# Three short gate/up pairs chained, and two more block products merged in the sixteen pairs after them

## The chip, the cores and the metric

The kernel runs on one core of a Trainium2 chip (trn2). The time is device microseconds from the start of an execution to its end. Engines are named as in the profile: PE (TensorE, matmul) with PEld (its weight loads), DVE (VectorE), ACT (ScalarE), POOL (GpSimd), SP (SyncE). PSUM is the accumulator memory that matmuls write; it has eight banks of 512 fp32 columns by 128 partitions, and the kernel allocates it in whole banks.

## The reference, cut to what matters

Two layers, each made of a first FFN, a token mix of three kinds of attention, and a second FFN, so four FFNs of one shape. All data are fp32.

```python
D_MODEL, SEQ, DEPTH, D_FF = 1024, 512, 2, 2816

def _swiglu(x, w1, w2):
    gt, up = jnp.split(x @ w1, 2, axis=-1)
    return (jax.nn.silu(gt) * up) @ w2

def reference(x, ...):
    for l in range(DEPTH):
        x = _layer_norm(DN_ALPHA * x + 0.5 * _swiglu(x, ffn1_w1[l], ffn1_w2[l]), ln1_g[l], ln1_b[l])
        mix = _token_mix(x, w_in[l], ...)
        x = _layer_norm(DN_ALPHA * x + mix, ln2_g[l], ln2_b[l])
        x = _layer_norm(DN_ALPHA * x + 0.5 * _swiglu(x, ffn2_w1[l], ffn2_w2[l]), ln3_g[l], ln3_b[l])
    return x
```

The change touches only `x @ w1` of `_swiglu`, followed by silu and the product.

## The kernel before, in words

**Precision.** An fp32 matmul is made of three in a rounded format (fp32r): every operand is split into a rounded part `hi` and a remainder `lo`, and hi·hi, hi·lo and lo·hi are added up in PSUM. ACT makes `hi` by a rounding copy (L160, L364, L369), DVE makes `lo` by a subtraction (L161, L365, L370). The activations `xx` (both parts, 512 tokens) stay in SBUF for a whole FFN; weights come by DMA as fp32 (`raw`) and are split as they come.

**One pair.** The first FFN product is computed in 22 pairs, f = 0 to 21: 128 gate columns and the 128 up columns that belong to them, for all 512 tokens. Pairs 0, 1 and 2 (`PLAIN`) are ordinary products (`proj`). From f = 3 on a pair is a 2x2 block product with seven block products in place of eight (Strassen's and Winograd's scheme): the tokens are cut into two halves of 256 (`H1`, `H2`), the 1024 inputs into two halves of four 128-row blocks. The left factors are sums and differences of weight blocks, made by DVE (`seven`, L348): g1 and g2 are the two halves of the gate weights, ua, ub, uc, ue and ud sums with the up weights. The right factors are blocks of the activations (p_, r_, s_) or of token sums (t1 to t4, tile `tz`). The products are named here by their left factors: P = g1·p_, then ua·t1, ub·t2, uc·t3, ud·t4, g2·r_ and ue·s_. The gate's first token half is P + g2·r_; the other three results share P and further sums.

**Two ways to run one block product.** `prod` (L402) issues twelve matmuls of 256 columns (four input blocks times hi·hi, hi·lo, lo·hi). `sided` (L410) lays the two parts of the right factor side by side: four matmuls of 512 columns give hi·hi in the first half of a bank and hi·lo in the second, then four of 256 columns add lo·hi to the first half. Its result lies in two halves that still have to be added (a "two-sided" sum); the diff calls this merged. Given two products, `sided` runs the 512s of the one, the 512s of the other, and then the 256s of both.

**Two ways to run a pair.** The short pairs f = 3, 4, 5 (below `HEAD` = 6, L341) go through `seven_products` (L419): three PSUM tiles, ga, pu and pv, each filled by two or one `prod`; sums are made by DVE (L432 to L439), partly from a copy `sn` that ACT makes (L428). No matmul there waits for a result of DVE or ACT of the same pair, except that g2 and ue at the end add to ga, which ACT copied long before. The sixteen pairs f = 6 to 21 go through `chained` (L442). There the running sum P + ub·t2 + ua·t1 + ue·s_ stays in one PSUM tile px, and its stages are copied out by ACT as they come: c1 after P (into half of the buffer t), cc after ub, the 512-wide cc after ua. uc and ud go to pw, g2 to py. ua, g2 and ue are merged, P, ub, uc and ud are not. ue and the evacuation of a pair are held back and run inside the next pair (`rest`, L482).

**Evacuation.** `evac` (L715) applies silu (ACT, L717) into one of two buffers t2[f % 2] and multiplies by the up half (DVE, L718). In `chained` the same buffer holds c1 until then.

**What sets the order.** PE's and POOL's instructions are issued in the order of the program text (`manual_schedule`, L89). DVE's and ACT's queues are ordered by a scheduler; copies and additions of `chained` have a raised priority there (L451, L455). An engine works through its queue in order, and waits between engines are derived from the tiles that the instructions read and write. PSUM tiles are taken in turn from a ring of eight banks (`ps`, L83): a tile gets the bank of the tile eight allocations earlier and waits until that has been read.

Of the kernel before, what the change touches and what calls it, by code (L numbers as in the profile page):

```python
# [10 lines left out]
F32 = mybir.dt.float32  # L11
F32R = mybir.dt.float32r
# [7 lines left out]
P = 128  # L20
S, D, F = 512, 1024, 2816
KD, KF, NB = D // P, F // P, S // P
# [44 lines left out]
def body(tc, a, out, depth=DEPTH):  # L67
# [13 lines left out]
    ring = [0]  # L81

    def ps(tag=None, name="ps", shape=(P, 512)):  # L83
        if tag is None:
            tag = PS_ALL[ring[0] % 8]
            ring[0] += 1
        return psp.tile(list(shape), F32, name=name, tag=tag, bufs=PS_TAGS[tag])
# [42 lines left out]
    nx = K()  # L130
# [210 lines left out]
    HEAD = 6  # L341
# [4 lines left out]
    H1, H2 = slice(0, 256), slice(256, 512)  # L346
# [55 lines left out]
    def prod(o, w, x, first=True):  # L402
        for k in range(4):
            hi, lo = w[0][:, k], w[1][:, k]
            vh, vl = x[0][:, k], x[1][:, k]
            for i, (wx, vx) in enumerate(((hi, vh), (hi, vl), (lo, vh))):
                nc.tensor.matmul(o, wx, vx, start=first and k == 0 and i == 0, stop=k == 3 and i == 2,  # L407
                                 skip_group_check=True)
# [30 lines left out]
        tt(ga[:, H2], ga[:, H2], v1, op=OP.add)  # L439
        return ga  # L440

    def chained(ws, tz, pl, u, held, end, t, evac):  # L442


        (g1, g2), (ua, ub, uc, ue), ud = ws
        (t1, t2, t3, t4) = [tz[:, i].rearrange("p k z s -> p z k s") for i in range(4)]
        two = lambda x: (x[:, 0], x[:, 1])
        p_, r_, s_ = [xx[:, :, k:k + 4, c] for k, c in ((0, H1), (4, H1), (4, H2))]

        def tt(*args):  # L450
            with tc.high_priority(100):  # L451
                nc.vector.tensor_tensor(*args, op=OP.add)

        def copy(o, x):
            with tc.high_priority(100):  # L455
                nc.scalar.activation(o, x, AF.Copy)  # L456

        px, pw, py = (ps(name=n) for n in ("px", "pw", "py"))
        cc = pl.tile([P, 768], F32, name="cc", tag="sn", bufs=1)
        prod(px[:, H1], g1, two(p_))  # L460
        c1 = t[:, H2]
        copy(c1, px[:, H1])
        prod(pw[:, H1], uc, two(t3))
        copy(pw[:, H2], pw[:, H1])
        if held:
            held.pop()()
        prod(px[:, H1], ub, two(t2), False)
        copy(cc[:, H1], px[:, H1])
        prod(pw[:, H1], ud, two(t4), False)
        y, x = (py, g2, r_, True), (px, ua, t1, False)  # L470
        if end:
            sided(x)
            sided(y)
        else:
            sided(y, x)
        copy(cc[:, 256:768], px)
        tt(c1, py[:, H2], c1)
        tt(py[:, H1], py[:, H1], c1)
        tt(u, pw, cc[:, 0:512])
        tt(u[:, H2], u[:, H2], cc[:, 512:768])  # L480

        def rest():  # L482
            sided((px, ue, s_, False))
            copy(t[:, H1], px[:, H2])
            tt(py[:, H2], px[:, H1], t[:, H1])
            evac(py)

        return rest

    def token_sums(k, tmp, th, tl):  # L490

# [213 lines left out]
    def ffn(l, w1, w2, which, xap, xa, wts, pend, done_prev, last, nxt, late=None):  # L705


        st = K()
        NA = KF - NTAIL
        plan = WIDE  # L710

        def hpart(f):
            return (st.ha, st.hb)[f >= NA][:, f - NA * (f >= NA)]

        def evac(f, pg, pu):  # L715
            t = st.t2[:, f % 2]
            g = nc.scalar.activation(t, pg, AF.Silu)  # L717
            st.last = g.ins, nc.vector.tensor_tensor(hpart(f), t, pu, op=OP.mult).ins  # L718

        hs, held = {}, []  # L720

        def h_parts(k, t):
            nc.scalar.activation(t[:, 0], hpart(k), AF.Copy)
            nc.vector.tensor_tensor(t[:, 1], hpart(k), t[:, 0].bitcast(F32), op=OP.subtract)
            hs[k] = t

        pts = staged(wts, pend)
        for tb in range(NB):
            nc.gpsimd.dma_start(x_sp[tb * P:(tb + 1) * P, :], xa[tb])
        done_prev()  # L730
        xap.release()
        st.w1p = nx.w1 = pool("w1p", side="right", reuse_waits="tile")
        more.n = 4
        with behind(lnq.sq):
            wp = [(wcols(w1, f * P), wcols(w1, F + f * P)) for f in PLAIN[2:]]

        for n, shape, dt, nb in (("hi", [P, KD, P], F32R, 2), ("lo", [P, KD, P], F32R, 2), ("ws", [P, KD, P], F32, 1),
                                 ("dh", [P, 4, P], F32R, 2), ("dl", [P, 4, P], F32R, 2), ("sn", [P, 768], F32, 1),
                                 ("v", [P, 256], F32, 1), ("raw", [P, KD, P], F32, 2)):
            st.w1p.tile(shape, dt, name=n, tag=n, bufs=nb)  # L740
        st.tz = st.w1p.tile([P, 4, 4, 2, 256], F32R, name="tz")
        th, tl = (st.tz[:, :, :, z] for z in range(2))
        tpl, nm, nb = (pre_t, "ws", 6) if late else (st.w1p, "raw", 2)
        lth = [token_sums(k, lambda: tpl.tile([P, KD, P], F32, name=nm, tag=nm, bufs=nb)
                          .rearrange("p a s -> p (a s)"), th, tl) for k in range(4)][-1]
        st.t = [(th[:, i], tl[:, i]) for i in range(4)]
        if late:
            late()
        fb = pool("fb", reuse_waits="tile")
        st.lnp = pool("lnp", reuse_waits="tile")  # L750
        st.t2 = st.lnp.tile([P, 2, S], F32, name="t2", tag="t2")
        fa = pool("fa", reuse_waits="tile")
        st.hb = fb.tile([P, NTAIL, S], F32, name="hb")
        st.ha = fa.tile([P, NA, S], F32, name="ha")

        ring[0] += 4
        for f in range(2, KF):
            if f not in PLAIN:
                ru = nx.w1.tile([P, KD, P], F32, name="raw", tag="raw", bufs=2) if f > 3 else None
                with behind(*(lth if f == PLAIN[-1] + 1 else lnq.parted if f < 6 else ())):  # L760
                    ws = seven(w1, f * P, F + f * P, nx.w1, ru, "half" if f < HEAD else "in place")
                with behind(*lnq.parted):
                    if f == PLAIN[-1] + 1:
                        evac(0, pts[0], pts[1])
                        evac(1, pts[2], pts[3])
                        for x in wp:
                            evac(*x)
                if f == KF - 1:
                    for k, n in zip(plan[1], ("hi", "lo")):
                        h_parts(k, wt.tile([P, KD, P], F32R, name=n, tag=n, bufs=3)  # L770
                                .rearrange("p (a b) c -> p a (b c)", a=2))
                if f < HEAD:
                    evac(f, seven_products(ws, st.t, nx.w1, hpart(f), 1), hpart(f))
                    continue
                held.append(chained(ws, st.tz, nx.w1, hpart(f), held, f == KF - 1, st.t2[:, f % 2], lambda p, f=f: evac(f, p, hpart(f))))
                if f == KF - 1:
                    held.pop()()
                continue
            wg, wu = wp.pop(0)
            pg, pu = ps(name="pg"), ps(name="pu")  # L780
            proj(pg, wg)
            proj(pu, wu)
            wp.append((f, pg, pu))
        nx.w1 = None
        st.w1p.tile([P, 88], F32, name="pad")
        st.w1p.release()
        accs = [[ps(name="acc") for _ in range(2)] for _ in range(NB)]
        short_rows(st, w2, accs, hs, h_parts, plan)
        xap, xa = alloc_xa(st.late if plan is WIDE else None)
        for tb in range(NB):  # L790
            nc.gpsimd.dma_start(xa[tb], x_sp[tb * P:(tb + 1) * P, :])
        hsp = pool("hsp", side="right", reuse_waits="tile")
        ln = LN(hsp, which, l, xa, 0.5, last)

        def wload(k):
            if k not in hs:
                h_parts(k, hsp.tile([P, 2, S], F32R, name="hs", tag="hs", bufs=5))
            return wrows(w2, k)

        wts, pend = rows_ln(KF, wload, lambda k: hs[k][:, 0], lambda k: hs[k][:, 1], ln, NA, fa.release, nxt,  # L800
                            plan[1][-1] + 1, accs)

        def done():
            nx_close()
            hsp.release()
            st.lnp.release()
            fb.release()

        return wts, pend, done, xap, xa
# [1145 lines left out]
    def late():  # L1955
        pre_t.release()
        tables(*tabs)
        init.release()
# [38 lines left out]
```

## Time and profile before

| | |
|---|---|
| runs | 2394.58, 2395.66, 2395.94 us; median 2395.66 |
| profiled execution | 2394.4 us; span of its instructions 2392.6 us |
| granted clock of TensorE | 0.999 of full speed |
| one FFN, three short pairs (899.9 to 930.1 us) | 30.2 us: PE 30.2 busy, DVE 26.3, ACT 14.6 |
| one FFN, sixteen pairs (930.1 to 1088.5 us) | 158.4 us: PE 158.4 busy, DVE 140.0, ACT 93.0 |

How to read it: times in the profile are us from the start of the span. A line such as `L407 PE MATMUL px<-xx,hi 128*128 128x256 f32 x12` is twelve matmuls of source line 407 that write tile px from xx and hi with 256 columns. What stands in brackets behind `<-` is the instruction that ended the idle time before. The chain that ended last is followed back from the last instruction; its pieces tell which engine sets the end at each moment. A matmul's length in the timeline (0.28 us for 256 columns) includes its way through the array; the distance from one start to the next is what it costs. The four FFNs begin their short pairs at about 49, 900, 1235 and 2087 us.

### The profile page before, as it was taken

What the parts mean: (1) busy time and instruction counts of PE and PEld (TensorE: products, weight loads), DVE (VectorE), ACT (ScalarE), POOL (GpSimd) and SP (SyncE); (2) the same over time, 40 slices, a digit from 0 to 9 for tenths busy, and PEclk for the clock granted to TensorE, in tenths of its full rate; (3) what the DMA queues carried; (4) which work ended last, traced back from release to release, by engine and by line L of the source; (5) the groups of instructions that cost most, each with busy time, mean ns of one, the idle gap of its engine ahead of it and who ended that gap; (6) DMA issues with size and microseconds to landing.
All of it is one profiled execution on the core that took longest, in us unless ns stands there. A gap on an engine that the chain in (4) does not pass through costs nothing.

```text
span 2392.6 us, 40932 instructions
## 1 busy us (share of the span) xinstructions
PE 2383.8 (100%) x15265; PEld 2113.8 (88%) x15265; DVE 1991.3 (83%) x3806; ACT 1326.6 (55%) x2537; POOL 344.6 (14%) x598
## 2 busy tenths in 40 slices
PE   9999999999999999999999999999999999999998
PEld 9999888888889989998899998878888898999987
DVE  7998975787688888998799989667777888999896
ACT  4565644577644545656445666445766445455563
POOL 2000312133321000001100002121333210000021
PEclk9999999999999999999999999999999999999999
DMA  6333975633165353437733349645322654433394
GB/s 205 109 111 103 243 203 160 177 95 87 45 160 140 115 161 110 116 103 207 203 116 111 110 140 207 197 131 153 99 78 60 158 135 149 125 106 110 102 237 142
DMA packets 407942, 330.23 MB, mean 138 GB/s; under 512 B 19208, under 2 KB 349336, under 8 KB 407744
## 3 DMA queue, kind: packets, MB, share of 16 engines
q1 hardware_dynamic: 380752, 261.83, 37.2%
q0 software_dynamic: 26992, 65.80, 11.9%
q8 instruction: 120, 1.97, 0.3%
q14 instruction: 78, 0.64, 0.1%
HBM read 300.26 MB, written 17.88 MB: 133 GB/s over the span
## 4 chain that ended last, share of the span: by engine, by line
PE 99%; DMA 0%; DVE 0%; POOL 0%; SPq 0%; issue 0%; POOLq 0%; ACT 0%; DVEq 0%
PE acc L574 13%; PE pw L407 8%; PE px L407 8%; PE acc L195 7%; PE pg L407 7%; PE pj L181 6%; PE pj L183 6%; PE pj L182 6%; PE px L414 5%; PE pu L407 3%; PE px L417 3%; PE py L414 2%; PE brp L182 2%; PE brp L181 2%; PE brp L183 2%; PE sN L1281 2%
## 5 line engine op out<-in xcount | busy, mean ns | idle before, releaser
L161 DVE TENSOR_TENSOR lo<-raw,hi 128x1024 fp32r<-128x1024 f32 x270 | 329.9, 1225 | 85.2 <-ACT hi L160 84.8
L160 ACT ACTIVATE hi<-raw 128x1024 fp32r<-128x1024 f32 x270 | 284.0, 1055 | 157.4 <-PE brp L182 36.3
L181 PE MATMUL pj<-xx,hi 128*128 128x512 f32 (+1 forms) x696 | 262.0, 376 | 0.2 <-ACT hi L1823 0.2
L183 PE MATMUL pj<-xx,lo 128*128 128x512 f32 (+1 forms) x696 | 250.5, 360 | 0.0
L182 PE MATMUL pj<-xx,hi 128*128 128x512 f32 (+1 forms) x696 | 250.5, 360 | 0.0
L574 PE MATMUL acc<-hi,xx 128*128 128x512 f32 x640 | 197.1, 389 | 0.0
L549 POOL DMA_DIRECT2D bt<-in_ffn_w_dram x32 | 40.4, 1273 | 935.6 <-DVE lo L161 935.3
L365 DVE TENSOR_TENSOR lo<-ws,hi 128x1024 fp32r<-128x1024 f32 x108 | 132.1, 1223 | 46.0 <-ACT hi L364 45.8
L183 PEld LDWEIGHTS pj<-xx,lo 128*128 128x128 f32 x696 | 131.5, 189 | 20.7 <-DVE lo L1824 0.2
L181 PEld LDWEIGHTS pj<-xx,hi 128*128 128x128 f32 x696 | 131.8, 189 | 16.2 <-issue 2.7
L182 PEld LDWEIGHTS pj<-xx,hi 128*128 128x128 f32 x696 | 132.2, 190 | 12.4 <-DVE xx L1909 0.2
L574 PEld LDWEIGHTS acc<-hi,xx 128*128 128x128 f32 x640 | 120.2, 188 | 24.9
L364 ACT ACTIVATE hi<-ws 128x1024 fp32r<-128x1024 f32 x108 | 114.1, 1056 | 49.3 <-DVE ws L387 15.8
L574 PE MATMUL acc<-lo,xx 128*128 128x512 f32 x320 | 124.6, 389 | 0.0
L407 PE MATMUL pg<-xx,hi 128*128 128x256 f32 x672 | 122.9, 283 | 0.0
L456 ACT ACTIVATE cc<-px 128x256 f32<-128x256 f32 (+1 forms) x128 | 62.5, 488 | 100.3 <-PE px L417 84.1
L407 PEld LDWEIGHTS pg<-xx,hi 128*128 128x128 f32 x672 | 106.2, 192 | 1.6
L456 ACT ACTIVATE t<-px 128x256 f32<-128x256 f32 x128 | 48.7, 380 | 84.4 <-PE px L407 47.0
L407 PE MATMUL pg<-xx,lo 128*128 128x256 f32 x336 | 95.2, 283 | 0.0
L407 PE MATMUL px<-xx,hi 128*128 128x256 f32 x512 | 94.9, 283 | 0.0
L407 PE MATMUL pw<-tz,hi 128*128 128x256 f32 x512 | 94.9, 283 | 0.0
L407 PE MATMUL pw<-tz,dh 128*128 128x256 f32 x512 | 94.9, 283 | 0.0
(482 smaller groups left out, 7184.1 us busy)
## 6 DMA issues: line engine op xcount, KB each, us to landing
raw<-in_ffn_w_dram SPq DMA_DIRECT2D x232, 512.0 KB, 3.9
raw<-in_w_in_dram SPq DMA_DIRECT2D x56, 512.0 KB, 4.0
raw<-in_w_gate_dram SPq DMA_DIRECT2D x48, 512.0 KB, 3.8
b<-in_ffn_w_dram SPq DMA_DIRECT2D x32, 512.0 KB, 7.4
bt<-in_ffn_w_dram POOLq DMA_DIRECT2D x32, 512.0 KB, 10.4
x_sp<-xa POOLq DMA_DIRECT2D x24, 512.0 KB, 6.5
xa<-x_sp POOLq DMA_DIRECT2D x24, 512.0 KB, 4.6
ks<-hl SPq DMA_DIRECT2D x96, 128.0 KB, 2.4
```

The source lines that it names most:

```text
L160: lnq.hi = nc.scalar.activation(hi[:, c], raw[:, c], AF.Copy).ins
L161: lnq.lo = nc.vector.tensor_tensor(lo[:, c], raw[:, c], hi[:, c].bitcast(F32), op=OP.subtract).ins
L181: nc.tensor.matmul(o, hi[:, k], vh, start=first, stop=False)
L182: nc.tensor.matmul(o, hi[:, k], vl, start=False, stop=False)
L183: nc.tensor.matmul(o, lo[:, k], vh, start=False, stop=last)
L195: nc.tensor.matmul(o, x(k)[:, t], y[:, c], start=first and i == 0, stop=last and i == 2, skip_group_check=True)
L364: pa = nc.scalar.activation(hi, x, AF.Copy)
L365: pv = tt(lo, x, hi.bitcast(F32), op=OP.subtract)
L407: nc.tensor.matmul(o, wx, vx, start=first and k == 0 and i == 0, stop=k == 3 and i == 2, skip_group_check=True)
L414: nc.tensor.matmul(o, w[0][:, k], x[:, :, k], start=first and k == 0, stop=False, skip_group_check=True)
L456: nc.scalar.activation(o, x, AF.Copy)
L574: nc.tensor.matmul(o[t], u[:, k, s], v[:, c], start=first and j == 0 and i == 0, stop=False, skip_group_check=True)
```

## The change

`seven_products` is no longer used by the FFN: f = 3, 4 and 5 go through `chained` too, with `merged=""`, so that all seven products are `prod`. There P and the running sum use the second half of the bank whose first half takes g2 (`x = px[:, H2]` with `px = py`), and one ring position is skipped. ACT copies c1 after P, cc after ub and after ua; ue then adds straight onto the second half, so that the held-back part has no copy and no addition. The order is P, g2, (ue and evacuation of the pair before), ub, uc, ua, ud.

For f = 6 to 21 `merged` is "AEGBP". P is merged (its copy c1 becomes 512 wide and fills t), and B (ub) is merged and issued in one `sided` call with ue of the pair before. Both copies of the running sum, after ub and after ua, are 512 wide and go to a 1024-wide cc. The gate's first half is folded from two-sided sums by `tt(c1, py, c1)` and `tt(py[:, H1], c1[:, H1], c1[:, H2])`; u gets two 512-wide additions. The tiles are taken in the order py, pw, px where it was px, pw, py. The order is P, uc, (ue of the pair before with B, its evacuation), ud, g2 with ua. The tiles `sn` (768) and `v` (256) give way to `cc` (1024).

```diff
-    def chained(ws, tz, pl, u, held, end, t, evac):
+    def chained(ws, tz, pl, u, held, t, evac, merged, end):
...
-        px, pw, py = (ps(name=n) for n in ("px", "pw", "py"))
-        cc = pl.tile([P, 768], F32, name="cc", tag="sn", bufs=1)
-        prod(px[:, H1], g1, two(p_))
-        c1 = t[:, H2]
-        copy(c1, px[:, H1])
-        prod(pw[:, H1], uc, two(t3))
+        def product(o, w, x, first=False):
+            prod(o, w, (x[:, 0], x[:, 1]), first)
+
+        py, pw = ps(name="py"), ps(name="pw")
+        if merged:
+            px = ps(name="px")
+        else:
+            px = py
+            ring[0] += 1
+        xc = H1 if merged else H2
+        x = px[:, xc]
+        cc = pl.tile([P, 1024], F32, name="cc", tag="cc", bufs=1)
+        sides = cc.rearrange("p (z i s) -> p z i s", z=2, i=2)
+        two = lambda y: y.rearrange("p (z s) -> p z s", z=2)
+        c1 = t if "P" in merged else t[:, H2]
+
+        def first():
+            if "P" in merged:
+                sided((px, g1, p_, True))
+                copy(c1, px)
+            else:
+                product(x, g1, p_, True)
+                copy(c1, x)
+
+        def last():
+            if not merged:
+                tt(py[:, H1], py[:, H1], c1)
+            elif "P" in merged:
+                tt(c1, py, c1)
+                tt(py[:, H1], c1[:, H1], c1[:, H2])
...
+            tt(u, pw, cc[:, 0:512])
+            if merged:
+                tt(u, u, cc[:, 512:1024])
+
+        if merged:
+            first()
+            product(pw[:, H1], uc, t3, True)
+            copy(pw[:, H2], pw[:, H1])
+            e = held.pop() if held else None
+            b = (px, ub, t2, False)
+            if e and e[0]:
+                sided(e[0], b)
+                e[1]()
+            else:
+                if e:
+                    e[1]()
+                sided(b)
+            copy(sides[:, :, 0], two(px))
+            product(pw[:, H1], ud, t4)
+            y, a_ = (py, g2, r_, True), (px, ua, t1, False)
+            if end:
+                sided(a_)
+                sided(y)
+            else:
+                sided(y, a_)
+            copy(sides[:, :, 1], two(px))
+            last()
+
+            def rest():
+                copy(t[:, H1], px[:, H2])
+                tt(py[:, H2], px[:, H1], t[:, H1])
+                evac(py)
+
+            held.append(((px, ue, s_, False), rest))
...
+            return
+        first()
+        product(py[:, H1], g2, r_)
+        if held:
+            held.pop()[1]()
+        product(x, ub, t2)
+        copy(cc[:, H1], x)
+        product(pw[:, H1], uc, t3, True)
         copy(pw[:, H2], pw[:, H1])
...
+        product(x, ua, t1)
+        copy(cc[:, H2], x)
+        product(pw[:, H1], ud, t4)
+        last()
 
         def rest():
-            sided((px, ue, s_, False))
-            copy(t[:, H1], px[:, H2])
-            tt(py[:, H2], px[:, H1], t[:, H1])
+            product(x, ue, s_)
             evac(py)
 
-        return rest
+        held.append((None, rest))
...
-                if f < HEAD:
-                    evac(f, seven_products(ws, st.t, nx.w1, hpart(f), 1), hpart(f))
-                    continue
...
+                chained(ws, st.tz, nx.w1, hpart(f), held, st.t2[:, f % 2], lambda p, f=f: evac(f, p, hpart(f)),
+                        "" if f < HEAD else "AEGBP", f == KF - 1)
```

More of the change, by code (lines that the diff above doesn't have):

```diff
@@ L440, in seven_products @@
         return ga
-    def chained(ws, tz, pl, u, held, end, t, evac):
+    def chained(ws, tz, pl, u, held, t, evac, merged, end):
         (g1, g2), (ua, ub, uc, ue), ud = ws
         (t1, t2, t3, t4) = [tz[:, i].rearrange("p k z s -> p z k s") for i in range(4)]
-        two = lambda x: (x[:, 0], x[:, 1])
         p_, r_, s_ = [xx[:, :, k:k + 4, c] for k, c in ((0, H1), (4, H1), (4, H2))]
@@ L456, in copy @@
                 nc.scalar.activation(o, x, AF.Copy)
-        px, pw, py = (ps(name=n) for n in ("px", "pw", "py"))
-        cc = pl.tile([P, 768], F32, name="cc", tag="sn", bufs=1)
-        prod(px[:, H1], g1, two(p_))
-        c1 = t[:, H2]
-        copy(c1, px[:, H1])
-        prod(pw[:, H1], uc, two(t3))
-        copy(pw[:, H2], pw[:, H1])
[L465 to L480, printed above, removed]
+        def product(o, w, x, first=False):
[6 more added lines that the diff above has]
+            ring[0] += 1
@@ new lines, in last @@
+        def last():
[5 more added lines that the diff above has]
+            else:
+                tt(c1, py[:, H2], c1)
+                tt(py[:, H1], py[:, H1], c1)
+            tt(u, pw, cc[:, 0:512])
[20 more added lines that the diff above has]
+                sided(y)
+            else:
+                sided(y, a_)
[6 more added lines that the diff above has]
+            held.append(((px, ue, s_, False), rest))
+            if end:
+                e = held.pop()
+                sided(e[0])
+                e[1]()
+            return
@@ L737, in ffn @@
         for n, shape, dt, nb in (("hi", [P, KD, P], F32R, 2), ("lo", [P, KD, P], F32R, 2), ("ws", [P, KD, P], F32, 1),
-                                 ("dh", [P, 4, P], F32R, 2), ("dl", [P, 4, P], F32R, 2), ("sn", [P, 768], F32, 1),
-                                 ("v", [P, 256], F32, 1), ("raw", [P, KD, P], F32, 2)):
+                                 ("dh", [P, 4, P], F32R, 2), ("dl", [P, 4, P], F32R, 2), ("cc", [P, 1024], F32, 1), ("raw", [P, KD, P], F32, 2)):
             st.w1p.tile(shape, dt, name=n, tag=n, bufs=nb)
@@ L771, in ffn @@
                                 .rearrange("p (a b) c -> p a (b c)", a=2))
-                if f < HEAD:
-                    evac(f, seven_products(ws, st.t, nx.w1, hpart(f), 1), hpart(f))
-                    continue
-                held.append(chained(ws, st.tz, nx.w1, hpart(f), held, f == KF - 1, st.t2[:, f % 2], lambda p, f=f: evac(f, p, hpart(f))))
-                if f == KF - 1:
-                    held.pop()()
+                chained(ws, st.tz, nx.w1, hpart(f), held, st.t2[:, f % 2], lambda p, f=f: evac(f, p, hpart(f)),
+                        "" if f < HEAD else "AEGBP", f == KF - 1)
                 continue
```

## The prediction

> **What bounds the kernel now.** The page first: span, busy line, chain of waits.
>
> ```profile
> span 2392.6 us, 40932 instructions
> PE 2383.8 (100%) x15265; PEld 2113.8 (88%) x15265; DVE 1991.3 (83%) x3806; ACT 1326.6 (55%) x2537; POOL 344.6 (14%) x598
> ...
> PE 99%; DMA 0%; DVE 0%; POOL 0%; SPq 0%; issue 0%; POOLq 0%; ACT 0%; DVEq 0%
> ```
>
> The matrix engine is busy without a break and is 99% of the chain that ended last. So the change can gain only by making the matmul stream itself shorter, and any wait that it puts into that stream is paid in full. The second view is therefore the chain in order of time, over one of the 64 pairs (16 in each of four FFNs) that the change merges further. Columns: start, length, line, count of matmuls.
>
> ```profile
> 958.74 1.44 PE px L407 x12
> 960.18 1.44 PE pw L407 x12
> 961.62 0.93 PE px L414 x4
> 962.55 0.47 PE px L417 x4
> 963.02 1.44 PE px L407 x12
> 964.45 1.44 PE pw L407 x12
> 965.89 0.93 PE py L414 x4
> 966.82 0.91 PE px L414 x4
> 967.73 0.47 PE py L417 x4
> 968.21 0.48 PE px L417 x4
> 968.69 1.44 PE px L407 x12
> ```
>
> In order: P (g1), uc, the last product ue of the pair before, B (ub), ud, then g2 and ua merged, and the next P. One pair takes 968.69 - 958.74 = 9.95 us. A plain product is twelve 256-column matmuls, 1.44 us, 0.12 each. A merged one is four 512-column and four 256-column matmuls: 0.93 + 0.47 = 1.40 us on the activations (xx), 0.91 + 0.48 = 1.39 on the token sums (tz). The third view is the same chain in the three short pairs ahead.
>
> ```profile
> 900.06 2.87 PE pg L407 x24
> 902.93 2.88 PE pu L407 x24
> 905.81 1.44 PE pv L407 x12
> 907.25 5.76 PE pg L407 x48
> 913.01 2.88 PE pu L407 x24
> ```
>
> Seven plain products back to back, 2.87 + 2.88 + 1.44 + half of 5.76 = 10.07 us; the matmul engine waits nowhere.
>
> **The merge in the 16 pairs.** P goes from 1.44 to 1.40 and B from about 1.435 (963.02 to 964.45 is 1.43) to 1.39; uc, ue, ud, g2 and ua keep their matmuls. The new pair is 1.40 + 1.44 + 1.40 + 1.39 + 1.44 + 2.79 = 9.86, so 0.09 less, and 64 x 0.09 = 5.8 us. That is the whole possible gain, 0.24%. The bounds are the rounding of these rows: 0.08 to 0.10, 5.1 to 6.4 us.
>
> The price of a matmul is what this hangs on. Four 256s of P (0.48) become two 512s' worth of time (0.93 / 2 = 0.465), so only what each matmul costs beyond its columns is saved. The Trainium skill, "TensorE: Matmul & The Clock Gate", section "Wait — 56ns, not 53.3ns?", says that a warm matmul costs its columns at 2.4 GHz and about 2.5 ns more. By that, merging away four matmuls saves an estimated 10 ns a product and 1.3 us over 128 products. It returns below beside a rival.
>
> What the merge adds beside the stream: the copy of P into t and the copy of B become 512 wide, and so do two additions. Groups by line, with the mean in ns:
>
> ```profile
> L364 ACT ACTIVATE hi<-ws 128x1024 fp32r<-128x1024 f32 x14 | 14.8, 1054 | 1.2 <-DVE ws L380 1.0
> ...
> L456 ACT ACTIVATE cc<-px 128x512 f32<-128x512 f32 x16 | 9.6, 598 | 25.9 <-PE px L417 25.9
> ...
> L456 ACT ACTIVATE cc<-px 128x256 f32<-128x256 f32 x15 | 5.7, 377 | 2.2 <-PE px L407 1.6 <-ACT t L456 0.7
> ```
>
> ```profile
> L452 DVE TENSOR_TENSOR ha<-pw,cc 128x512 f32<-128x512 f32 x12 | 8.2, 683 | 0.1
> L452 DVE TENSOR_TENSOR t<-py,t 128x256 f32<-128x256 f32 x16 | 6.7, 420 | 3.5 <-PE py L417 3.4
> ...
> L452 DVE TENSOR_TENSOR ha<-ha,cc 128x256 f32<-128x256 f32 x12 | 5.0, 416 | 0.0
> ```
>
> ScalarE gets 2 x (0.598 - 0.377) = 0.44 us a pair, VectorE 2 x 0.265 = 0.53. How much room they have is one row of the windows over 14 pairs:
>
> ```profile
> core 0: us, PE busy (x) PEld busy (x) DVE busy (x) ACT busy (x) POOL busy (x), PEclk, DMA share, GB/s
> ...
> 938.68:1078.11 139.43, 139.43 (x1010) 132.00 (x1009) 127.58 (x183) 82.81 (x139) 0.00 (x0) 1.00 0.37 110
> ```
>
> VectorE is busy 127.58 / 14 = 9.11 us a pair and would be busy 9.64 of 9.86; ScalarE goes from 5.9 to 6.4. No DMA is added or moved, and cc takes the memory of sn and v. ScalarE's addition is hidden by its own idle time. VectorE's is hidden only while 0.2 us a pair are left; that is the second rival.
>
> Some waits exist already. Where the copy of B was late, the matmul engine waited for it (start, length, engine, line):
>
> ```profile
> 978.52 0.40 PE L407 MATMUL px<-xx,hi 128*128 128x256 f32 x2
> ...
> 985.56 0.78 PEld L414 LDWEIGHTS py<-xx,hi 128*128 128x128 f32 x4
> 985.68 1.09 PE L414 MATMUL py<-xx,hi 128*128 128x512 f32 x4
> ...
> 986.17 0.37 ACT L456 ACTIVATE cc<-px 128x256 f32<-128x256 f32 x1
> ...
> 986.60 0.77 PEld L414 LDWEIGHTS px<-tz,hi 128*128 128x128 f32 x4 [0.26 <-ACT cc L456]
> ...
> 986.96 0.59 ACT L717 ACTIVATE t<-py 128x512 f32<-128x512 f32 x1
> ```
>
> and in the chain
>
> ```profile
> 986.77 1.03 PE px L414 x4
> ```
>
> The copy ended at 986.54, the next weight load began at 986.60, and the group took 1.03 instead of 0.91: 0.12 us lost. With a copy longer by 0.22 the same lateness loses about 0.34. A second one is new: the tiles are now taken in the order py, pw, px from eight banks, so a pair's px gets the bank of py two pairs back, which is free only after that pair's silu. Here the silu starts 986.96 - 978.52 = 8.4 us after P's first matmul. It follows ue, whose end the merge moves back by the 0.91 of B's 512s, so it would end at 8.4 + 0.9 + 0.6 = 9.9, against a pair of 9.86. A few pairs would lose some 0.2 us. I take 0.8 us in all for both, with 0 and 3 as ends, since most copies come in time. The merge alone is then -5.8 + 0.8 = -5.0 us.
>
> **The three short pairs.** They keep 84 matmuls of 0.12 us, so nothing is gained on the path. VectorE loses five additions and gets two, which is worth nothing while it is not waited for. What is new is the order: P into the second half of py, copy c1 out of it by ScalarE, then g2 into the first half of the same tile. In the code nothing of g2 depends on c1. But whether the halves count as separate, a row shows:
>
> ```profile
> 914.05 0.69 DVE L390 TENSOR_TENSOR raw<-raw,ws 128x512 f32<-128x512 f32 x1
> 916.00 0.42 DVE L432 TENSOR_TENSOR v<-pu,sn 128x256 f32<-128x256 f32 x1 [1.26 <-PE pu L407]
> ```
>
> v reads only the first half of pu. That half was complete 12 matmuls after 913.01, at about 914.5, and VectorE stood idle from 914.74, yet v began at 916.00, just after the second half (915.89). A reader thus waits for a write to the other half of its tile. I take it that a writer waits for a reader likewise; no row shows that direction. The Trainium skill, "PSUM — Partial Sum Buffer", section "PSUM bank collisions raise a hardware error", speaks against this change here: it counts a read by ScalarE and a write by TensorE in one bank as a collision whichever columns they touch, and tells authors to guard by bank.
>
> The price of one such wait, from f = 6, whose P and c1 are plain now too:
>
> ```profile
> 931.57 0.40 PE L407 MATMUL pw<-tz,hi 128*128 128x256 f32 x2
> ...
> 931.83 0.38 ACT L456 ACTIVATE t<-px 128x256 f32<-128x256 f32 x1 [0.51 <-PE px L407]
> ```
>
> The next product begins at 931.57, the copy of P at 931.83 and ends at 932.21: 0.64 after. From a copy's end to the weight load it is 0.06 (986.54 to 986.60), from there to the matmul 0.12 (985.56 to 985.68). So 0.64 + 0.06 + 0.12 = 0.82 us, in three pairs of four FFNs: 12 x 0.82 = 9.8 us. The low end is a copy that starts at once, 0.56 each, 6.7 us; the high end, half of the copies behind a weight split that has just begun on ScalarE (1.05), 9.8 + 6 x 1.05 = 16 us. I take 0.82, since in the row ScalarE stood waiting for the copy. Behind the waiting g2 stands the whole matmul queue.
>
> One of the 12 costs more. c1 goes to half of the buffer t, which an earlier pair's silu and product use:
>
> ```profile
> 48.78 0.40 PE L407 MATMUL pg<-xx,hi 128*128 128x256 f32 x2
> ...
> 50.20 1.28 DVE L718 TENSOR_TENSOR ha<-t,pj 128x512 f32<-128x512 f32 x2
> ```
>
> In the first FFN, P of the first short pair ends at 48.78 + 1.44 = 50.22, but the product that reads t ends at 51.48. The copy then ends at about 51.9, and the wait is 1.9 instead of 0.82: 1.1 us more. The other copies of the short pairs have a product of 1.44 us ahead of the matmul that needs them, more than 0.82, and cost nothing.
>
> **Sum.** -5.8 + 0.8 + 9.8 + 1.1 = +5.9 us. The profiled execution is 2394.4 us (span 2392.6, 1.8 around it), so 2400.3; it lies 1.3 below the median of 2395.66, and against that median the sum gives 2401.6 us, 0.25% slower. What this measurement can tell from no change is about 0.2%, 4.8 us: below 2390.9 is faster, above 2400.5 slower. With the ends named, this case runs from 2397 (0.56 a wait, nothing else late) to 2409.
>
> **The rivals.**
> *Halves are separate for a writer* (not slower). If g2 does not wait for c1, the 9.8 and the 1.1 go: c1 then has g2, 1.44 us, as cover. The result is 2395.7 - 5.0 = 2390.7, on the edge of faster. For it: no row shows a writer waiting. Against it: the row of v. It decides as soon as the matmul after the short P starts 0.12 after the last one. 22%.
> *VectorE becomes the bound.* At 9.64 of 9.86 us it has almost no slack, and it takes its work in order. If half of its present idle time of (139.43 - 127.58) / 14 = 0.85 us stays as waiting in order, a pair lasts 9.64 + 0.42 = 10.06, 0.2 more than its matmuls, in 14 x 4 pairs 11 us; with the short pairs' part even 2412. It decides once splits of the next pair are late at its P. Against it: an engine that is behind arrives later and waits less, and the short pairs give VectorE some time back. 15%.
> *Merging saves hardly anything.* If P and B as 512s cost as much as their 256s, because the stream has to step between two stretches of xx or because weight loads set the pace, the 5.8 us go and the time is 2407.4. It decides when four 512s reach 0.96. The rows of 0.93 and 0.91, of products merged the same way already, speak against it: 5%. By the estimate from the Trainium skill's page "TensorE: Matmul & The Clock Gate" above it would be 2401.6 + 5.8 - 1.3 = 2406; the trace disagrees with that page, with 0.04 to 0.05 us a product where it gives 0.01.
>
> **How the numbers follow.** The likeliest case has 58% and gives 2401.6; of it 36 points lie above 2400.5 and 22 within 0.2%. Separate halves: 22%, 12 faster and 10 the same. VectorE 15% and the dear merge 5%, slower. Faster 0.12, same 0.32, slower 0.56. The likeliest case's own range is 2397 to 2409; to hold 8 in 10 it must reach down to the separate halves, 2390, and up to 2410, which leaves out most of the VectorE case and the lowest of the separate halves.
>
> **What would show it.** Right: in the short pairs an idle time of 0.7 to 0.9 us ahead of g2, 12 times, released by ScalarE's copy into t, and one near 1.9 in the first FFN; in the 16 pairs 9.86 from P to P. Wrong: g2 following P without a gap (first rival); pairs of 10 us and more with waits on splits or additions (second); pairs still at 9.95 without waits (third); silu ahead of P's waits in many pairs, which I priced at nearly nothing.

## The result

The changed kernel takes 2409.82 us (median of 6 runs, 2408.73 to 2410.37) and the kernel before 2394.48 (6 runs beside them, 2393.81 to 2395.94): ratio 1.0063, 95% interval 1.005 to 1.0076. That is 15.3 us slower. The profiled executions differ by the same: span 2408.1 against 2392.6.

The page of the profile after, its first lines and the line of the chain by engine:

```profile
span 2408.1 us, 39973 instructions
...
PE 2383.7 (99%) x14753; PEld 2085.1 (87%) x14753; DVE 2018.3 (84%) x3770; ACT 1365.4 (57%) x2573; POOL 345.4 (14%) x598
...
PE 11%; DVE 2%; ACT 1%; issue 0%; POOL 0%; POOLq 0%; DVEq 0%; ACTq 0%
```

There are 512 matmuls fewer, 4 in each of 128 products. The busy time of PE hardly fell, because part of each wait counts as busy: a matmul's recorded length (0.28 us) reaches beyond the 0.12 after which the next can start, so that a wait of 0.63 shows as 0.47 idle in the timeline below. The chain could be followed back over 11% of the span only, so it is no use here. What PE waited for is the better view (what waited, for what: us in total, times, longest). After:

```profile
PE py L407 <- ACT t L455: 9.3, 12, 2.5
PE px L414 <- ACT cc L455: 3.0, 8, 0.5
PE py L407 <- ACT cc L455: 1.6, 1, 1.6
PE pj L181 <- ACT hi L1876: 1.2, 1, 1.2
...
PE pw L407 <- ACT pw L455: 0.3, 2, 0.2
```

and before, where beside one wait at the kernel's very start this is all:

```profile
PE pj L181 <- ACT hi L1823: 0.2, 1, 0.2
```

The 12 waits of py for t are the ones that were forecast, g2 behind the copy c1 out of its own bank: one in each short pair of each feed-forward network (FFN). Three other kinds of wait for a ScalarE copy are there too.

By stage, from the first matmul of the short pairs to the first after the sixteenth merged pair, as the matmuls' starts give it:

| us | FFN 0 | FFN 1 | FFN 2 | FFN 3 | sum |
|---|---|---|---|---|---|
| before | 189.56 | 189.57 | 189.57 | 189.57 | 758.27 |
| after | 194.75 | 192.63 | 192.25 | 193.78 | 773.41 |

These stages hold 15.1 of the 15.5 us between the spans. Another 0.3 is at the start of the kernel (pj behind hi), ahead of the first short pair; elsewhere the two traces run alike. Within the stages the matmul gaps of the short pairs add up to 15.0 us, and the sixteen merged pairs come out even.

One nominal wait, timeline of after (start, length, engine, line, operation, and in brackets the idle time and what ended it):

```profile
927.69 0.28 PE L407 MATMUL py<-xx,lo 128*128 128x256 f32 x1
928.44 0.50 PE L407 MATMUL py<-xx,hi 128*128 128x256 f32 x2 [0.47 <-ACT t L455]
...
928.00 0.38 ACT L455 ACTIVATE t<-py 128x256 f32<-128x256 f32 x1 [0.92 <-PE py L407]
```

g2 should have started 0.12 after 927.69. It starts 0.06 after the copy's end (928.38), 0.63 late, and its first two matmuls take 0.50 together where 0.40 is usual: 0.73 in all.

A merged pair that nothing disturbs, same view:

```profile
967.54 1.09 PE L414 MATMUL px<-xx,hi 128*128 128x512 f32 x4
968.47 0.63 PE L417 MATMUL px<-xx,lo 128*128 128x256 f32 x4
968.94 0.40 PE L407 MATMUL pw<-tz,hi 128*128 128x256 f32 x2
...
977.40 0.86 PE L414 MATMUL px<-xx,hi 128*128 128x512 f32 x3
```

From P to P it is 977.40 - 967.54 = 9.86 us, and P's parts are 0.93 (to 968.47) and 0.47. But three pairs of every FFN are longer: 10.61, 10.40 and 10.14 to 10.17. The longest, with ScalarE's queue behind it:

```profile
961.80 1.06 ACT L160 ACTIVATE hi<-raw 128x1024 fp32r<-128x1024 f32 x1
962.77 0.36 ACT L455 ACTIVATE t<-px 128x256 f32<-128x256 f32 x1
963.03 1.05 ACT L364 ACTIVATE hi<-raw 128x1024 fp32r<-128x1024 f32 x1
963.98 1.05 ACT L160 ACTIVATE hi<-raw 128x1024 fp32r<-128x1024 f32 x1
964.93 0.59 ACT L455 ACTIVATE cc<-px 128x512 f32<-128x512 f32 x1
...
964.00 1.09 PE L414 MATMUL py<-xx,hi 128*128 128x512 f32 x4
965.57 1.19 PE L414 MATMUL px<-tz,hi 128*128 128x512 f32 x4 [0.48 <-ACT cc L455]
```

Two splits of L160 stand in ScalarE's queue here, and the clean pair after it has none. Four pairs of each FFN carry two such splits, and the three late ones are among them; the pairs with one or none are not late. The copy of B comes last behind them, and ua, due 0.93 after 964.00, starts 0.64 late and loses 0.10 more at its start.

### The profile page after: what moved, and what is told of

Read it like the earlier page. It is cut to its first block, busy times and chain, and to the rows that moved or that the text cites. A ratio compares the mean times of both kernels' runs of the same rounds, so it can differ in the third digit from the quotient of the medians.

```text
span 2408.1 us, 39973 instructions
## 1 busy us (share of the span) xinstructions
PE 2383.7 (99%) x14753; PEld 2085.1 (87%) x14753; DVE 2018.3 (84%) x3770; ACT 1365.4 (57%) x2573; POOL 345.4 (14%) x598
## 5 line engine op out<-in xcount | busy, mean ns | idle before, releaser
L161 DVE TENSOR_TENSOR lo<-raw,hi 128x1024 fp32r<-128x1024 f32 x270 | 330.5, 1227 | 89.8 <-ACT hi L160 89.4
L160 ACT ACTIVATE hi<-raw 128x1024 fp32r<-128x1024 f32 x270 | 283.5, 1054 | 156.2 <-PE brp L182 36.3
L364 ACT ACTIVATE hi<-ws 128x1024 fp32r<-128x1024 f32 x108 | 114.4, 1059 | 48.8 <-DVE ws L387 15.4
L414 PE MATMUL px<-tz,hi 128*128 128x512 f32 x512 | 139.0, 393 | 3.0 <-ACT cc L455 3.0
L414 PE MATMUL px<-xx,hi 128*128 128x512 f32 x512 | 139.8, 394 | 0.0
L455 ACT ACTIVATE cc<-px 128x512 f32<-128x512 f32 x128 | 76.1, 595 | 95.3 <-PE px L417 94.3
L414 PEld LDWEIGHTS px<-tz,hi 128*128 128x128 f32 x512 | 94.7, 188 | 28.1 <-ACT cc L455 8.2
L407 PE MATMUL pw<-tz,dh 128*128 128x256 f32 x608 | 112.9, 283 | 0.3 <-ACT pw L455 0.3
L407 PE MATMUL pw<-tz,hi 128*128 128x256 f32 x608 | 112.2, 282 | 0.0
L365 DVE TENSOR_TENSOR lo<-raw,hi 128x1024 fp32r<-128x1024 f32 x76 | 92.8, 1221 | 18.9 <-ACT hi L364 18.9
L455 ACT ACTIVATE t<-px 128x512 f32<-128x512 f32 (+1 forms) x128 | 62.3, 486 | 68.7 <-PE px L417 48.2
```

The costliest lines, as they stand in the source:

```text
L160: lnq.hi = nc.scalar.activation(hi[:, c], raw[:, c], AF.Copy).ins
L161: lnq.lo = nc.vector.tensor_tensor(lo[:, c], raw[:, c], hi[:, c].bitcast(F32), op=OP.subtract).ins
L364: pa = nc.scalar.activation(hi, x, AF.Copy)
L365: pv = tt(lo, x, hi.bitcast(F32), op=OP.subtract)
L414: nc.tensor.matmul(o, w[0][:, k], x[:, :, k], start=first and k == 0, stop=False, skip_group_check=True)
```

## The experiments

The kernel before was run beside each; its medians lie between 2394.28 and 2394.68. The two theories at the start: the loss is g2 waiting for the copy in its own bank (the forecast); or the sixteen pairs lose as well, to VectorE or to the merge itself.

**The short pairs back to before, the merged sixteen kept.**

```diff
+                if f < HEAD:
+                    evac(f, seven_products(ws, st.t, nx.w1, hpart(f), 0), hpart(f))
+                    continue
```

> Short pairs f = 3 to 5 back to the seven separate products, the sixteen pairs merged as in the change. Theory (the short pairs carry the whole loss, 15.0 us of the 15.5 us between the two spans, because g2 waits for the copy out of its own bank, and the sixteen pairs come out even): 2394 to 2396 us; if the three late copies of an FFN come from a backlog that the short pairs leave, they go as well and it is 2388 to 2390. Rival (the loss comes from the sixteen pairs, VectorE or their copies): still above 2404.

Here `seven_products` keeps its copy and the sum v in the tile cc instead of the tiles sn and v; its short pairs take 30.2 us an FFN as before.

2399.43 us, ratio 1.002 (1.001 to 1.0029): between the two. So most of the loss is the short pairs' own, but the merge alone, which I had put at 5 us of gain, costs 4.9. What PE waits for:

```profile
PE pw L407 <- DVE lo L365: 3.9, 3, 1.3
PE px L414 <- ACT t L459: 1.7, 2, 0.8
...
PE px L414 <- ACT cc L459: 0.7, 2, 0.5
```

The products wait for VectorE's half of a weight split (lo) and for late copies out of px.

**The short pairs as changed, the sixteen as before.**

```diff
+                if f < HEAD:
+                    chained(ws, st.tz, ..., "", False)
+                else:
+                    chained_old(ws, st.tz, ...)
```

> Short pairs as in the change, the sixteen pairs as before (P and B plain). Theory: the short pairs alone cost 15 us, 2409 to 2411 us. Rival (the merge in the sixteen pairs is to blame): 2394 to 2398.

2410.90 us, ratio 1.007 (1.0055 to 1.0085): the short pairs alone carry 16.4 us, in the profiled execution 1.2 of it through a slower clock behind the longest wait (the last section shows it). PE's waits are those of the changed kernel without the late copies out of px:

```profile
PE py L407 <- ACT t L455: 8.8, 12, 2.5
PE py L407 <- ACT cc L455: 2.3, 2, 1.3
```

The two halves of the change cost 4.9 and 16.4 by themselves and 15.3 together. They don't add up, since each moves the order of VectorE's and ScalarE's work, and so which copy is late.

**The running sum of the short pairs in a bank of its own, same order.**

```diff
-            px = py
-            ring[0] += 1
+            px = ps(name="px")
...
-        product(py[:, H1], g2, r_)
+        product(py[:, H1], g2, r_, True)
...
+            copy(py[:, H2], x)
```

> As the change, but in the short pairs the running sum lies in a third bank and not in the bank of g2; same order of the products, and one 256-wide copy more at the evacuation, off the path. Theory (bank): the twelve waits ahead of g2 (11.2 us in the trace) go, apart from about 1.4 us in the first FFN where the copy comes later than g2 can cover; the waits for a late copy ahead of ua and ud (about 2.5 us) stay: 2399 to 2401 us. Rival (the copy is late for its data, the bank does not matter): the waits move to ub, and it stays at 2406 to 2410.

2396.18 us, ratio 1.0009 (1.0 to 1.0018): 13.6 us come back, more than I expected. All 12 waits ahead of g2 are gone; what is left are late copies:

```profile
PE px L414 <- ACT cc L455: 2.9, 8, 0.5
...
PE px L407 <- ACT t L455: 1.1, 1, 1.1
```

The last is in the first FFN, where ub and not g2 is now the next product that needs the copy; it shows that c1 comes late there whatever stands behind it.

**The same bank, with uc between the copy and g2.**

```diff
         first()
+        product(pw[:, H1], uc, t3, True)
+        copy(pw[:, H2], pw[:, H1])
         product(py[:, H1], g2, r_)
...
-        product(pw[:, H1], uc, t3, True)
-        copy(pw[:, H2], pw[:, H1])
+        product(pw[:, H1], ud, t4)
```

> As the change, but the order in the short pairs is P, uc, g2, (ue before), ub, ud, ua: the bank of P and g2 is shared as in the change, and uc, 1.44 us into another bank, stands between. Theory (bank, and only the neighbourhood of P and g2): the waits of 0.63 to 1.1 us are covered, the first FFN keeps about 1.3 us: 2398 to 2401 us. Rival (copy late for its data): 2406 to 2410.

2394.17 us, ratio 0.9998 (0.9989 to 1.0008): even with the kernel before, 15.7 us under the change. PE's waits for copies:

```profile
PE py L407 <- ACT t L455: 1.4, 1, 1.4
...
PE py L407 <- ACT cc L455: 0.8, 1, 0.8
```

Eleven of the twelve waits are gone without another bank. A product of 1.44 us into another bank is cover enough; so the price was not the copy, but that g2 stood directly behind it. Not all of the 15.7 us is this, however: by the matmuls' starts the short pairs give back 11.4, and 3.6 come from the sixteen merged pairs, which were not edited. Their late copies cost about 0.3 twice in each FFN, and 0.15 a third time in three of the four, where in the change they cost 0.74, 0.53 and 0.28.

**The copy c1 issued twice.**

```diff
                 copy(c1, x)
+                copy(c1, x)
```

> The changed kernel with the first block product's copy of the short pairs issued twice (12 more copies of 256 columns, 0.28 to 0.38 us each on ScalarE, out of the bank that g2 writes). Bank theory: g2 waits for the second copy too, each of the 12 waits grows by 0.3 to 0.4 us, and the time goes from 2409.8 to 2413 to 2415. Rival (the wait ends with something other than the copy): 2409 to 2411.

2415.43 us, ratio 1.0089 (1.0075 to 1.0102): 5.6 more than the change. The nominal waits grew from 0.63 to 1.05, and the long one of the first FFN from 2.70 to 3.12; the middle ones, 1.10 before, have no split ahead of their two copies now and take 1.05. One such wait:

```profile
930.82 0.80 ACT L455 ACTIVATE t<-py 128x256 f32<-128x256 f32 x2 [0.92 <-PE py L407]
...
930.50 0.28 PE L407 MATMUL py<-xx,lo 128*128 128x256 f32 x1
931.67 0.50 PE L407 MATMUL py<-xx,hi 128*128 128x256 f32 x2 [0.89 <-ACT t L455]
```

The copies end at 931.62 and g2 starts 0.05 later, though its own half of the tile was never copied. With the two runs before, this shows that g2 waits for every copy out of the other half. Whether the bank makes it wait, or the way in which this program derives its waits from tiles, no run tells apart, since a PSUM tile is a whole bank in all of them. The sum of all waits rose by 3.6 us only, since the middle ones did not grow; 1.5 more are a stretch at a slower clock in the first FFN.

**Less work on VectorE, in the merged sixteen alone and in the whole change.** Both leave out the second addition of the up sum.

```diff
-            if merged:
-                tt(u, u, cc[:, 512:1024])
```

First with the short pairs of before:

> The kernel with short pairs as before and the merged sixteen, with the second addition of the up sum left out in the sixteen pairs (64 additions of 512 columns; this part of the sum is missing from the output). Theory that VectorE's load makes the merge come out even: without 64 x 0.66 us on VectorE the weight splits come earlier, the waits of ua and uc for VectorE's lo and for late copies shrink, and the time falls from 2399.4 to 2389 to 2393. Rival theory (the loss is the two-sided products' own, on TensorE, or ScalarE's queue alone): 2398 to 2400.

2392.5 us, ratio 0.9992 (0.9983 to 1.0001): 6.9 us less than with the addition. The waits for lo are gone. The addition was also a reader of cc, but in neither trace does a copy into cc wait for VectorE, so the effect is put down to the load. Then in the changed kernel:

> The changed kernel with the second addition of the up sum left out in the sixteen pairs (64 additions of 512 columns on VectorE; that part of the sum is missing from the output), nothing put in its place. Theory that VectorE's load takes the merge's gain and that the short pairs' loss is the bank's own: the late copies of the sixteen pairs (1.6 us a feed-forward) shrink to 0.7 or less as they did with the short pairs of before, 3.6 us or more in all, and the nine waits ahead of g2 that are at 0.63 stay at 0.63, so 2403.5 to 2406.2. If VectorE also sets the bank waits: under 2402. If the late copies are ScalarE's queue alone: 2409 to 2411.

2407.85 us, ratio 1.0057 (1.0043 to 1.007): 2.0 us less, about halfway between the theories. Two of the three late pairs of each FFN become clean or lose 0.2, some 3 us in all; the first keeps its 0.64. The waits ahead of g2 hardly follow VectorE: ten of the twelve stay within 0.03 us, one in FFN 2 falls from 1.10 to 0.69 and one in FFN 3 from 0.71 to 0.63. In FFN 2 ua now waits 1.30 for a late copy; in the change it did so in FFN 3 alone. In the profiled execution 1.3 us go back to a slower clock in the first FFN. The late copy that is left:

```profile
961.56 1.06 ACT L160 ACTIVATE hi<-raw 128x1024 fp32r<-128x1024 f32 x1
962.53 1.04 ACT L364 ACTIVATE hi<-raw 128x1024 fp32r<-128x1024 f32 x1
963.48 1.04 ACT L160 ACTIVATE hi<-raw 128x1024 fp32r<-128x1024 f32 x1
...
964.68 0.59 ACT L455 ACTIVATE cc<-px 128x512 f32<-128x512 f32 x1
```

Three splits follow each other without a gap on ScalarE, then the copies out of px. The split ahead of these (L364 of ws, at 960.40) had itself waited 0.32 us for VectorE's ws. With uc between, where the addition is still on VectorE, ws is begun 0.92 us after P instead of 2.47, ahead of two other additions, and the same pair takes 9.86 to 10.02 instead of 10.62. So VectorE's load makes two of the three copies late; the third goes with the order of the work on VectorE and ScalarE, which was not varied by itself.

**The second addition given to GpSimd instead**, in the kernel with uc between, and in the change.

```diff
-                tt(u, u, cc[:, 512:1024])
+                nc.gpsimd.tensor_tensor(u, u, cc[:, 512:1024], op=OP.add)
```

> The kernel with uc between the copy and g2 in the short pairs, with the second addition of the up sum in the sixteen pairs (64 of 512 columns, SBUF alone) given to GpSimd, which has no work in this stage. Theory that VectorE's load is what makes copies late: the two late copies of a feed-forward (0.27 each) and the waits of FFN0 and FFN1 for copies behind late weight splits shrink, as leaving these additions out did; the waits left are 2.4, 1.5, 0.9 and 0.9 us in the four feed-forwards, so at most 5.7 us are to be had; I take half to all: 2388.5 to 2391.5. Rival (the product with silu waits for GpSimd, whose addition takes 2 us or more by its rows of 1.08 us for 256 columns, or VectorE slows beside it): 2394 to 2400.

> The changed kernel with the same 64 additions given to GpSimd and nothing else. Theory (short pairs' bank waits are their own, merge's gain is eaten by VectorE's load): the late copies of the sixteen pairs (1.6 us a feed-forward) shrink to 0.5 or less, so 4 to 6 us come back, and the waits ahead of g2 stay: 2404 to 2406. Rival (the bank waits' size also follows VectorE): below 2403; or GpSimd's addition is itself late: 2409 or more.

2401.91 us, ratio 1.0031 (1.0019 to 1.0044), and 2415.67, ratio 1.0088 (1.0075 to 1.0102): both lose, 7.7 us over the kernel with uc between and 5.9 over the change (1.4 of these a slower clock in the first FFN). In the first, VectorE is busier with 0.69 us of additions a pair taken away than with them (windows: us, PE, PEld, DVE, ACT, POOL):

```profile
938.68:1078.11 139.43, 138.24 (x890) 124.87 (x889) 138.23 (x167) 88.20 (x139) 24.95 (x14) 1.00 0.35 104
```

In the kernel with uc between DVE has 134.25 there. One line has grown, here in its groups by line:

```profile
L381 DVE TENSOR_TENSOR raw<-raw,ws 128x512 f32<-128x512 f32 x14 | 24.2, 1731 | 0.2
```

and in the kernel with uc between

```profile
L381 DVE TENSOR_TENSOR raw<-raw,ws 128x512 f32<-128x512 f32 x14 | 9.6, 683 | 0.0
```

The timeline of the first shows why:

```profile
965.58 1.22 DVE L380 TENSOR_TENSOR ws<-raw 128x1024 f32<-128x1024 f32 x1
966.83 1.67 DVE L381 TENSOR_TENSOR raw<-raw,ws 128x512 f32<-128x512 f32 x1
...
965.75 2.21 POOL L493 TENSOR_TENSOR ha<-ha,cc 128x512 f32<-128x512 f32 x1 [8.95 <-DVE ha L451]
```

GpSimd starts while VectorE adds (L380, to 966.80) and ends 1.16 after that. VectorE's next addition ends at 968.50, 0.54 after GpSimd's, as if it had begun only then (alone it takes 0.68). GpSimd additions that start during a VectorE addition of 0.43 us last 1.40, and those that start while VectorE does nothing 1.29; so the 2.21 us hold a wait. The Trainium skill, "SBUF — State Buffer", section "SBUF: two separate sides", says that VectorE and GpSimd lock a shared pair of ports for a whole instruction when VectorE has two inputs in SBUF; these rows agree. VectorE saved 0.69 a pair and lost 1.05.

**c1 in another place, another order, and the last two products one after the other.** Three more kernels, all from the one with uc between. c1 stands in the half of u that is written last, alone and then with the pair before's product moved behind ub; and with this second version, py's whole product ahead of ua's:

```diff
-        c1 = t if "P" in merged else t[:, H2]
+        c1 = t if "P" in merged else u[:, H1]
...
-                sided(y, a_)
+                sided(y)
+                sided(a_)
```

> The kernel with uc between the copy and g2, with the first block product's copy in the half of u that is written last, and the order otherwise as there (the product of the pair before stays ahead of ub). It parts the two edits that were made together at 2399.6. If the place was harmless and the order cost the 5 us: 2392.5 to 2394, with the wait of 1.57 us in the first feed-forward down to 0.8. If the place cost it: 2398 to 2400.

> The changed kernel with two edits in the three short pairs of a feed-forward: the order P, uc, g2, ub, the product of the pair before, ud, ua, and the copy of the first block product put into the half of u that is written last, so that it no longer waits for the silu's buffer. The bank theory (a product waits while ScalarE copies out of the bank that it writes; a product of another bank of 1.44 us in between covers it): the waits ahead of g2 stay at 0 as with uc in between, the one of 1.4 us in the first feed-forward goes with the buffer, and the time is 2394.2 less 1.4 to 2.2, so 2391.5 to 2393. Rival (the first feed-forward's wait belongs to ScalarE's queue and not to the buffer): the wait stays ahead of some product and the time stays at 2393.5 to 2395.

> The kernel of the two edits in the short pairs, and in the sixteen pairs the two products at the end one after the other, py's whole ahead of ua's, instead of by turns. Theory that the late copy out of px costs the merge its gain (ua waits 0.17 to 0.64 us three times in a feed-forward): py's product of 0.93 us lies whole between the copy and ua, 0.47 us more cover than now, so the waits shrink by up to 1.3 us in a feed-forward, 5 in all, and the time is 2387 to 2390. Rival (by turns two matmuls share one load of the weights, or the order sets the clean pair's length): the clean pair grows over 9.86 us and the time is the same as or above the kernel with the two edits alone.

2396.66 us (ratio 1.001, 1.0001 to 1.0019), 2399.6 (1.0022, 1.0013 to 1.0031) and 2412.62 (1.0075, 1.0062 to 1.0089). All three miss what was expected. With c1 alone moved, the first FFN's wait shrinks from 1.57 to 0.77 as expected, but uc now waits in every FFN for a split of VectorE:

```profile
PE pw L407 <- DVE lo L365: 2.0, 4, 0.9
```

With the order moved as well, the late copies of 0.64, 0.43 and 0.17 return. One after the other, the clean pair is 9.87, so it costs no more on TensorE. But in each FFN two pairs lose 1.1 to 1.4 us ahead of ub or ua, two more 0.3 to 0.4, and uc waits 1.44 for lo in a fifth:

```profile
PE pw L407 <- DVE lo L365: 7.2, 8, 1.3
PE px L414 <- ACT cc L455: 4.5, 4, 1.1
PE px L414 <- ACT t L455: 3.3, 4, 0.8
```

Each edit moves the places that the splits get in the two queues, and with VectorE busy for 96% of this stage in the changed kernel some split comes late. No whole version beats the kernel before; the one with uc between equals it.

## Why the prediction was right in its direction and too small in its size

The forecast was 5.9 us slower, the measurement 15.3. The time of 2409.82 lies inside the stated range, 2390 to 2410, by 0.2 us, and above the 2409 of the likeliest case. There was luck in that: the range was laid from a kernel before of 2395.66 us, and beside the change it took 2394.48; as a difference the range ended at 14.3.

**Every wait is paid in full**: right. The sums of the gaps in the matmul stream and of the lost time agree to 0.1 us.

**The clean pair, 9.86 us**: right to the hundredth in 11 of the 15 distances from P to P of every FFN (the first pair takes 9.90, since the short pair's ue ahead of it is not merged; three are late), and with it the price of a 512-column matmul. The rival by the page "TensorE: Matmul & The Clock Gate" of the Trainium skill, an estimated pair of 9.93, falls: P's four 512s took 0.93, as quoted above.

**"I take 0.8 us in all for both ... since most copies come in time"**: this step failed, the largest miss. Most copies did come in time, but the three late ones lose 0.74, 0.53 and 0.28 in each FFN, 6.2 us in all, and that is the whole gain. The merge was put at -5.0 and came out at 0. I had looked at room by the mean over 14 pairs, while the lateness arises in three of the four pairs that carry two splits of L160. The second part of the term, px waiting for the silu of two pairs back, did not occur in this kernel.

**g2 waits for the copy in its bank**: right in kind, place and number. The nominal wait is 0.73 instead of 0.82 in six of the 12, and 0.80 and 0.82 in two more. Two steps inside it were too low. In three FFNs the middle short pair waits 1.10 plus 0.10, because its copy stood behind a split that ScalarE had just begun; that case I had named, but only as the high end. In the first FFN it is 2.80 instead of 1.9. Here ScalarE's queue at that place:

```profile
50.83 1.06 ACT L160 ACTIVATE hi<-raw 128x1024 fp32r<-128x1024 f32 x1
51.77 0.63 ACT L369 ACTIVATE dh<-raw 128x512 fp32r<-128x512 f32 x1
52.29 0.60 ACT L775 ACTIVATE t<-pg 128x512 f32<-128x512 f32 x1
52.77 0.39 ACT L455 ACTIVATE t<-py 128x256 f32<-128x256 f32 x1
```

The buffer was free at 51.78, when the product of L776 ended, but the copy had two splits and a silu ahead of it. All 12 together cost 12.4 us against 10.9 in the forecast.

**"The other copies of the short pairs ... cost nothing"**: failed. I compared the cover with the copy's own length, not with where the copy stands in ScalarE's queue. It cost 2.6 us, most of it in one place of the last FFN:

```profile
2103.93 1.06 ACT L364 ACTIVATE hi<-raw 128x1024 fp32r<-128x1024 f32 x1 [2.97 <-DVE raw L390]
2104.89 1.04 ACT L160 ACTIVATE hi<-raw 128x1024 fp32r<-128x1024 f32 x1
2105.84 0.36 ACT L455 ACTIVATE cc<-py 128x256 f32<-128x256 f32 x1
...
2106.26 0.50 PE L407 MATMUL py<-tz,hi 128*128 128x256 f32 x2 [1.62 <-ACT cc L455]
```

ScalarE stood idle for 2.97 us, waiting with a split for VectorE, while the copy that ua needs was queued behind that split. ua came 1.78 late.

**The sum.** 1.5 more for the bank waits, 2.6 for the other copies, 5.0 for the merge and 0.3 at the start make 9.4, which with the forecast's 5.9 is the measured 15.3.

**The rivals.** Halves that are separate for a writer: refuted in this kernel, by the trace and by the copy issued twice. A dear merge: refuted. VectorE as the bound: not in its form, as no run of pairs takes 10.06. But its core was nearer than the 15% I gave it: leaving out 0.69 us a pair on VectorE brought 6.9 us with the short pairs of before, and 2.0 in the whole change, where 1.3 more went to the slower clock. What stays open is why the place of a buffer or the order of two products decides which split is late; I saw that it does, not by what rule.

## What to carry to other kernels

In this kernel a matmul that wrote into a PSUM tile directly behind a copy out of that tile waited for the whole copy, though it wrote other columns; putting the products in another order, so that one into another bank stood between, took 11 of 12 such waits away. When a copy is costed at nothing because a product covers it, look at where it stands in its engine's queue and for whom the instructions ahead of it wait, in the fullest pair and not in the mean one. On a matmul stream without gaps a saving of 0.09 us a pair is given back by a single copy every eighth pair that comes as late as the worst here (0.74).

## What the runs showed of the hardware that was not expected

- After a stall the matmul stream loses 0.10 us more: the first two 256-column matmuls take 0.50 instead of 0.40, and four of 512 columns 1.19 instead of 1.09. It came back with every one of the changed kernel's 27 waits in these stages.
- After the longest wait the clock was lower for a while, in some kernels. The windows of the changed kernel without the second addition, and then of the changed kernel, show it in the first FFN (the column ahead of the last two is the granted clock):

```profile
53.00:57.00 4.00, 3.99 (x21) 3.99 (x22) 3.84 (x6) 0.90 (x1) 0.00 (x0) 0.58 0.02 4
```

```profile
53.00:57.00 4.00, 3.79 (x31) 3.79 (x32) 4.00 (x6) 1.49 (x3) 0.00 (x0) 1.00 0.04 12
```

  Both had stood still for 2.5 us, until about 53. In the first 14 matmuls then took 0.21 us each instead of 0.12, 1.3 us more; in the second none did. The profiles of the short pairs alone, of c1 copied twice and of the change with GpSimd show 13 to 16 such matmuls at the same place; kernels without this stall show none. A stall of this length thus cost half as much again in four of five profiles, and nothing more in the fifth; what decides is not shown.
- A 512-column addition on GpSimd lengthened the addition of VectorE beside it from 0.68 to 1.73 us, so that handing it over made VectorE busier.
